# Sums of down-projection weights held behind an addition of a later unit, and spread over fourteen units

## The chip, the cores and the metric

One NeuronCore of a Trainium2 chip runs the whole kernel as one launch. The metric is the device time of that launch in microseconds. The kernel before takes 1783.04 us, the median of three runs (1782.25 to 1786.08).

## What is computed

One layer of a decoder on 1024 tokens of width 1024, in float32: a norm and a combined projection, two attention branches, their gated sum, a SwiGLU block with 2816 hidden features, a gated embedding and a last norm. The change lies in the SwiGLU block:

```python
n2 = rms_norm(h, g_ffn[i])
h = h + (jax.nn.silu(n2 @ w_ffn_gate[i]) * (n2 @ w_ffn_up[i])) @ w_ffn_down[i]
```

## The kernel before

Every product in float32 is made of three matmuls on a high and a low half of each operand (`passes`, lines 134 to 139: high by high, high by low, low by high). `split` (lines 130 to 132) makes the halves: ScalarE casts the high half (line 131), VectorE subtracts it from the source to give the low half (line 132). So the third matmul of a product, line 139, is the first that needs VectorE's work on that weight.

The SwiGLU block uses the Winograd form of a 2 by 2 block product: seven products of sums of blocks in place of eight. For the gate and up projections the hidden features come in 22 units of 256, here numbered 0 to 21: even ones are columns of the gate, odd ones the same columns of the up projection. `wino` builds a unit: GpSimd makes the sums of weight blocks (`s1`, and in place in `raw`; lines 958, 959, 975, 977), each of the seven weight operands is split into a tile `wl` (three buffers), and each of the seven products i is a group of twelve matmuls into a bank of PSUM named `pP`, `pR` or `pQ`. Behind a group, ScalarE copies the bank (`snap`) or VectorE adds it to an earlier copy (`add`, line 968). From unit 3 on the products come in the order 1, 5, 2, 6, 7, 3, 4; the addition behind product 7 reads `pP`, that behind product 3 reads `pQ`.

A gate unit ends in SiLU on ScalarE. An up unit multiplies (GpSimd at line 1023, or VectorE at line 1025), and then VectorE makes four subtractions for the down projection (`sub`, line 1016), which wait for GpSimd's product; all seven results go to DRAM (`d_g`, line 1013). The first three units work on operands `b` that VectorE still splits at the stage's start.

The down projection runs after the 22 units and needs, for each of its eleven block rows kk (KK is 11), four sums of weight blocks too. They are made during the units: `down_in(kk)` loads four blocks of 128 by 512 into one half of the buffer `spare` (line 1102, four DMAs of 256 KB), and `down_sums(kk)` makes the four sums on VectorE (line 1109), each followed by a store to DRAM (`d_w`, line 1110). The two halves of `spare` alternate, so the load of block kk + 2 waits for the stores of block kk. Earlier, `spare` holds other tiles. At the end, eight direct blocks are loaded into it (line 1131).

All these loads and stores are issued from SP's queue, where the loads of the units' raw weights (line 830, 1 MB each, three buffers) and the stores of `d_g` stand too. The code calls `down_in` in one turn of a loop over units 3 to 21 and `down_sums` in the next, but the order of the code is not the order of issue: a scheduler that works with modelled times puts each instruction on its engine's list as soon as what it needs is there, unless a priority or `tc.issue_after` says otherwise.

Of the kernel before, what the change touches and what calls it, by code (L numbers as in the profile page):

```python
# [14 lines left out]
ALU = mybir.AluOpType  # L15
# [36 lines left out]
def decoder_layer(ctx: ExitStack, tc: tile.TileContext, x, p, positions, g_mix, w_in, g_q_a, w_q_b,  # L52
                  g_kv_a, w_kv_b, w_br_mla, w_br_sb, w_out, g_ffn, w_ffn_gate, w_ffn_up, w_ffn_down,
                  w_ple_gate, w_ple_proj, g_ple, g_final, xT, pT, out):
    nc = tc.nc
# [101 lines left out]
    with ExitStack() as att:  # L157
# [17 lines left out]
        with ExitStack() as sb:  # L175
# [111 lines left out]
            with ExitStack() as p2:  # L287
# [18 lines left out]
                kk = rp.tile([P, S], F32, name="kk")  # L306
# [28 lines left out]
            for k2 in range(NK // 2):  # L335
# [4 lines left out]
                for t in range(NT):  # L340
                    s = slice(t * P, (t + 1) * P)
# [135 lines left out]
            for pr in range(HEADS // 2):  # L477
                kst, q1, q2 = cur
                oT = wp.tile([P, S], F32, name="oT", tag="oT", bufs=1)
                for a in range(2):  # L480
# [5 lines left out]
                                            op=ALU.subtract)  # L486
# [346 lines left out]
    def gate_up_raw(u):  # L833
        return raw_unit((w_ffn_gate, w_ffn_up)[u % 2], u // 2)
# [111 lines left out]
    t1_factors(quarter[0], bc0)  # L946
    acc = out_group(1, 2, 2)

    FIRST = (1, 2, 5, 6, 7, 3, 4)
    firsts = iter((M, O, B))  # L950
    ORDER = (1, 5, 2, 6, 7, 3, 4)

    def wino(raw, order, ctile, ready):

        a11, a12, a21, a22 = [raw[:, kh * 4:kh * 4 + 4, f * P:(f + 1) * P] for f in range(2) for kh in range(2)]
        s1 = wk.tile([P, 4, P], F32, name="s1", tag="c", bufs=4)
        G = nc.gpsimd
        G.tensor_tensor(out=s1, in0=a21, in1=a22, op=ALU.add)
        G.tensor_tensor(out=a21, in0=a11, in1=a21, op=ALU.subtract)
        left = {1: a11, 2: a12, 3: a12, 4: a22, 5: s1, 6: a11, 7: a21}  # L960
        bank, s = {}, {}

        def snap(key, pt):
            s[key] = ctile()
            nc.scalar.copy(out=s[key], in_=pt)

        def add(key, pt):
            nc.vector.tensor_tensor(out=s[key], in0=pt, in1=s[key], op=ALU.add)  # L968
            return s[key]

        for n, i in enumerate(order):
            w = wk.tile([P, 2, 4, P], F32R, name="wl", tag="wl", bufs=3)
            split(w[:, 0], w[:, 1], left[i])
            if i == 1:
                G.tensor_tensor(out=a11, in0=s1, in1=a11, op=ALU.subtract)
            elif i == 2:
                G.tensor_tensor(out=a12, in0=a12, in1=a11, op=ALU.subtract)
            k = "P" if i in (1, 6, 7, 4) else "R" if i == 2 else "Q"
            first = k not in bank
            if first:  # L980
                spec = B if k == "R" else next(firsts) if k == "Q" and order is FIRST else A
                bank[k] = ps.tile([P, HALF], F32, name="p" + k, **spec)
            pt = bank[k]
            passes(pt, [((w[:, 0, kk, :], w[:, 1, kk, :]), (Bn[i][:, 0, kk, :], Bn[i][:, 1, kk, :]))
                        for kk in range(4)], first=first, last=i in (2, 3, 4), skip_group_check=True)
            if i in (1, 6):
                snap(i, pt)
            elif i == 2:
                ready(0, 0, add(1, pt))
            elif i == 3:  # L990
                ready(0, 1, add(6, pt))
            elif i == 4:
                ready(1, 0, None, pt)
            elif (12 - i) in s:
                ready(1, 1, add(12 - i, pt))
            else:
                snap(i, pt)
            yield
# [80 lines left out]
    def rest():  # L1079
        global_sl = sl  # L1080
        nxt = gate_up_raw(3)
        for u in range(3, NFF):
            raw = nxt
            if u + 1 < NFF:
                nxt = gate_up_raw(u + 1)
            if u % 2:
                yield up_unit(u // 2, raw, ORDER, t_tile, global_sl)
            else:
                global_sl = {}
                yield gate_unit(raw, ORDER, t_tile, global_sl)  # L1090

    KK = NFF // 2
# [5 lines left out]
    def down_in(kk):  # L1098

        a = {(f, kh): spare[:, 4 * (kk % 2) + 2 * f + kh, :] for f in range(2) for kh in range(2)}  # L1100
        for (f, kh), t in a.items():
            nc.sync.dma_start(out=t, in_=down_block(f, kh, kk))
        return a

    def down_sums(kk, a):

        for i, dst, x, y, op in ((5, (1, 1), (1, 0), (1, 1), ALU.add), (7, (1, 0), (0, 0), (1, 0), ALU.subtract),
                                 (6, (0, 0), (1, 1), (0, 0), ALU.subtract), (3, (0, 1), (0, 1), (0, 0), ALU.subtract)):
            nc.vector.tensor_tensor(out=a[dst], in0=a[x], in1=a[y], op=op)
            nc.sync.dma_start(out=d_w[LEFT[i], kk], in_=a[dst])  # L1110
# [2 lines left out]
    DIRECT = {1: (0, 0), 2: (0, 1), 4: (1, 1)}  # L1113
    before = None
    blocks = {}
    for n, u in enumerate(rest()):

        if 2 <= n < KK + 2:
            blocks[n - 2] = down_in(n - 2)
        for _ in range(2):  # L1120
            next(u)
        for _ in before or ():
            pass
        for _ in range(3):
            next(u)
        before = u
        if 3 <= n < KK + 3:
            down_sums(n - 3, blocks.pop(n - 3))
        if n == KK + 4:
            for kk in range(0, 8, 2):  # L1130
                nc.sync.dma_start(out=spare[:, kk:kk + 2, :], in_=wd[0, :, kk:kk + 2, hcol(0)])

# [75 lines left out]
    for hf, c0, n in ((1, 0, 4), (0, 0, 2), (0, 2, 2)):  # L1208
        c = slice(c0 * P, (c0 + n) * P)
        w_ = slice(0, n * P)  # L1210
        s = slice(hf * HALF + c0 * P, hf * HALF + (c0 + n) * P)
# [67 lines left out]
```

## Time and profile before

| | |
|---|---|
| time, median of three runs | 1783.04 us |
| the profiled execution | 1785.67 us |
| its span, first to last instruction | 1784.0 us |
| mean granted clock of TensorE | 0.981 |
| TensorE busy (matmuls) | 1697.2 us, 95% |
| VectorE busy | 1157.2 us, 65% |
| ScalarE busy | 901.7 us, 51% |
| GpSimd busy | 389.7 us, 22% |
| gate and up units | about 1000 to 1451 us of the span |

In the profile PE is TensorE, PEld its weight loads, DVE VectorE, ACT ScalarE, POOL GpSimd and SP the queue of SyncE. A line such as L1109 is a line of the kernel. A row of a timeline gives the start in the span, the duration, the engine, the line, the operation, and out<-in with sizes; brackets give the idle time ahead of it and what ended it. In the view of waits a row gives the waiting instruction, what it waited for, the total in us, the times and the longest. The clock is a share of full speed.

### The profile page before, as it was taken

The page shows a single profiled execution, that of the slowest core. Times are in us where ns is not written, and L with a number is a line of the kernel's source. Part 1 is how long each engine was busy: PE and PEld are TensorE (multiplying, and loading weights), DVE is VectorE, ACT ScalarE, POOL GpSimd, SP SyncE. Part 2 cuts the span into 40 slices and gives each one's busy share as a digit, 9 for nine tenths or more (in the row PEclk, how much of TensorE's full clock was granted, in tenths as well). Part 3 has the DMA queues.
Part 4 walks back from the last instruction along what each step waited for, and adds up shares of the span by engine and source line. Part 5 has one row for each costly group of instructions (what it writes and reads, how often), then busy time and mean ns, then how long its engine had stood idle before and what let it go on. Part 6 is the DMA issues. An engine that isn't in the chain of part 4 may idle for free.

```text
span 1784.0 us, 23325 instructions
## 1 busy us (share of the span) xinstructions
PE 1697.2 (95%) x8148; PEld 1410.5 (79%) x8148; DVE 1157.2 (65%) x2063; ACT 901.7 (51%) x1748; POOL 389.7 (22%) x401
## 2 busy tenths in 40 slices
PE   6999999999998999996999899899999999999996
PEld 5888878888786888885889777688888878887795
DVE  6667788778885766686468765754444545557656
ACT  5266676767774777775335633233333334445411
POOL 2011320000210533342202623334434310000000
PEclk9999999999999999998999899999999999999998
DMA  5212221213314210215953475853223328565522
GB/s 171 55 58 48 59 60 42 82 45 90 115 42 138 72 61 31 83 58 200 346 205 115 143 257 180 277 168 100 95 89 118 113 101 300 191 198 164 165 67 79
DMA packets 168249, 222.16 MB, mean 125 GB/s; under 512 B 23170, under 2 KB 99970, under 8 KB 168130
## 3 DMA queue, kind: packets, MB, share of 16 engines
q1 hardware_dynamic: 162098, 200.73, 34.6%
q0 software_dynamic: 6032, 19.93, 3.1%
q8 instruction: 64, 1.05, 0.2%
q14 instruction: 55, 0.45, 0.1%
HBM read 151.93 MB, written 67.90 MB: 123 GB/s over the span
## 4 chain that ended last, share of the span: by engine, by line
PE 74%; DVE 9%; issue 6%; DMA 5%; POOL 2%; ACT 2%; SPq 1%; POOLq 0%; DVEq 0%; ACTq 0%
PE pt L137 5%; PE pt L138 5%; PE pt L139 5%; PE pd L138 4%; PE pd L137 4%; PE pd L139 4%; PE pP L139 3%; PE pP L137 3%; PE pP L138 3%; DMA spare<-w_ffn_down 2%; PE po L137 2%; PE tp L651 2%; PE po L138 2%; PE po L139 2%; PE pg L139 2%
## 5 line engine op out<-in xcount | busy, mean ns | idle before, releaser
L137 PE MATMUL pt<-nTh,w_h 128*128 128x512 f32 (+1 forms) x480 | 192.5, 402 | 3.4 <-ACT go L355 2.4
L138 PE MATMUL pt<-nTl,w_h 128*128 128x512 f32 (+1 forms) x480 | 190.1, 396 | 0.0
L139 PE MATMUL pt<-nTh,w_l 128*128 128x512 f32 (+1 forms) x480 | 189.0, 395 | 0.0
L132 DVE TENSOR_TENSOR wl<-raw,wl 128x512 fp32r<-128x512 f32 x132 | 95.4, 723 | 101.9 <-ACT wl L131 101.4
L139 PE MATMUL pP<-b,wl 128*128 128x512 f32 x352 | 139.8, 399 | 10.1 <-DVE wl L132 10.1
L131 ACT CAST wl<-raw 128x512 fp32r<-128x512 f32 x132 | 82.0, 622 | 129.2 <-PE pP L139 59.0
L137 PE MATMUL pP<-b,wl 128*128 128x512 f32 x352 | 140.2, 398 | 5.0 <-DVE t L968 3.2
L138 PE MATMUL pP<-b,wl 128*128 128x512 f32 x352 | 139.3, 396 | 0.0
L137 PEld LDWEIGHTS pt<-nTh,w_h 128*128 128x128 f32 (+1 forms) x480 | 90.7, 189 | 26.1 <-ACT go L355 5.8
L139 PEld LDWEIGHTS pt<-nTh,w_l 128*128 128x128 f32 (+1 forms) x480 | 90.6, 189 | 19.7
L138 PEld LDWEIGHTS pt<-nTl,w_h 128*128 128x128 f32 (+1 forms) x480 | 90.9, 189 | 18.5
L138 PE MATMUL pd<-drs,dls 128*128 128x512 f32 x296 | 102.0, 390 | 1.0 <-DVE drs L132 1.0
L139 PE MATMUL pd<-drs,dls 128*128 128x512 f32 x296 | 101.7, 389 | 0.0
L132 DVE TENSOR_TENSOR drs<-drr,drs 128x512 fp32r<-128x512 f32 x74 | 50.8, 690 | 78.1 <-ACT drs L131 78.1
L137 PE MATMUL pd<-drs,dls 128*128 128x512 f32 x296 | 100.7, 392 | 0.4 <-ACT dls L131 0.4
L131 ACT CAST drs<-drr 128x512 fp32r<-128x512 f32 x74 | 45.9, 623 | 105.0 <-PE pd L139 98.3
L637 POOL TENSOR_SCALAR pw<-pw,st 128x128 f32<-128x128 f32 (+5 forms) x48 | 75.0, 1569 | 71.6 <-DVE st L633 20.2
L139 PEld LDWEIGHTS pP<-b,wl 128*128 128x128 f32 x352 | 67.4, 192 | 28.2 <-DVE wl L132 13.9
L137 PEld LDWEIGHTS pP<-b,wl 128*128 128x128 f32 x352 | 67.7, 192 | 20.1 <-DVE t L968 4.1
L138 PEld LDWEIGHTS pP<-b,wl 128*128 128x128 f32 x352 | 67.6, 192 | 14.3
L445 DVE TENSOR_TENSOR sz<-sz,T 128x512 f32<-128x512 f32 (+2 forms) x96 | 52.2, 550 | 34.6 <-PE T L443 33.8
L356 POOL DMA_DIRECT2D d_gate<-go x32 | 17.8, 556 | 260.3 <-ACT go L355 221.2
(371 smaller groups left out, 4821.9 us busy)
## 6 DMA issues: line engine op xcount, KB each, us to landing
d_g<-t SPq DMA_DIRECT2D x74, 256.0 KB, 2.0
drr<-d_g SPq DMA_DIRECT2D x74, 256.0 KB, 2.8
w_raw<-w_in SPq DMA_DIRECT2D x33, 512.0 KB, 4.2
raw<-w_ffn_gate SPq DMA_DIRECT2D x11, 1024.0 KB, 5.6
raw<-w_ffn_up SPq DMA_DIRECT2D x11, 1024.0 KB, 5.5
spare<-w_ffn_down SPq DMA_DIRECT2D x44, 256.0 KB, 3.7
d_w<-spare SPq DMA_DIRECT2D x44, 256.0 KB, 3.6
drr<-d_w SPq DMA_DIRECT2D x44, 256.0 KB, 2.6
```

Source lines behind the costliest of these rows:

```text
L131: nc.scalar.copy(out=h, in_=src)
L132: eng.tensor_tensor(out=l, in0=src, in1=r32(h), op=ALU.subtract)
L137: nc.tensor.matmul(ps, lhsT=ah, rhs=bh, start=first and i == 0, stop=False, **kw)
L138: nc.tensor.matmul(ps, lhsT=ah, rhs=bl, start=False, stop=False, **kw)
L139: nc.tensor.matmul(ps, lhsT=al, rhs=bh, start=False, stop=last and i == n - 1, **kw)
L356: nc.gpsimd.dma_start(out=dst, in_=go[0:rows, :])
L445: nc.vector.tensor_tensor(out=sz[:, c0:], in0=sz[:, c0:], in1=T[:, c0:], op=ALU.subtract)
L637: nc.gpsimd.tensor_scalar(out=pw[:, 0:nk], in0=pw[:, 0:nk], scalar1=st[:, 6:7], scalar2=None, op0=ALU.mult)
L651: nc.tensor.transpose(tp[:, i * P:(i + 1) * P], rows[i][:, kb * P:(kb + 1) * P], ident)
```

## The change

The four sums of a block are no longer free to be issued when their loads have landed: they are held behind the latest addition (`add`) that the code had made at that point, which is the one behind product 7 of the unit of that turn. And the blocks are called in at other turns: n counts the turns from 0 (unit 3), and the new table `when` puts the loads of kk = 0 to 10 at turns 2, 3, 4, 5, 7, 8, 9, 10, 12, 13, 14, and the sums one turn later, in place of turns 2 to 12 and 3 to 13. The last loads into `spare` are called one turn later. The kernel gets three lines longer, so lines behind the first edit have moved by one, and those behind the loop by three.

```diff
+    latest = {}
...
         def add(key, pt):
-            nc.vector.tensor_tensor(out=s[key], in0=pt, in1=s[key], op=ALU.add)
+            latest["add"] = nc.vector.tensor_tensor(out=s[key], in0=pt, in1=s[key], op=ALU.add).ins
             return s[key]
...
+    when = {2 + 5 * kk // 4: kk for kk in range(KK)}
     for n, u in enumerate(rest()):
-        if 2 <= n < KK + 2:
-            blocks[n - 2] = down_in(n - 2)
+        if n in when:
+            blocks[when[n]] = down_in(when[n])
...
-        if 3 <= n < KK + 3:
-            down_sums(n - 3, blocks.pop(n - 3))
-        if n == KK + 4:
+        if n - 1 in when:
+            with tc.issue_after(latest["add"]):
+                down_sums(when[n - 1], blocks.pop(when[n - 1]))
+        if n == KK + 5:
```

What it moves is seen in the engines' lists. First VectorE in units 0 to 2, up to the split for product 2 of unit 1, `wl_9915` (`b3` is an operand, `pR_9900` the bank of unit 0). Before:

```order
L132 TENSOR_TENSOR b3_9246<-t_9047,b3_9246 128x512
L1109 TENSOR_TENSOR spare_9084<-spare_9084 128x512
L132 TENSOR_TENSOR b3_9246<-t_9051,b3_9246 128x512
L132 TENSOR_TENSOR b3_9246<-t_9055,b3_9246 128x512
L968 TENSOR_TENSOR spare_9084<-pR_9900,spare_9084 128x512
L132 TENSOR_TENSOR b3_9246<-t_9059,b3_9246 128x512
L1109 TENSOR_TENSOR spare_9084<-spare_9084 128x512
L132 TENSOR_TENSOR wl_9915<-raw_9706,wl_9915 128x512
```

And now:

```order
L132 TENSOR_TENSOR b3_9246<-t_9047,b3_9246 128x512
L132 TENSOR_TENSOR b3_9246<-t_9051,b3_9246 128x512
L132 TENSOR_TENSOR b3_9246<-t_9055,b3_9246 128x512
L969 TENSOR_TENSOR spare_9084<-pR_9900,spare_9084 128x512
L132 TENSOR_TENSOR b3_9246<-t_9059,b3_9246 128x512
L132 TENSOR_TENSOR wl_9915<-raw_9706,wl_9915 128x512
```

The two sums ahead of that split are gone. The same goes for all sums in units 0 to 5: on VectorE's list the first sum now stands behind the addition after product 7 of unit 6.

Second, VectorE in unit 7, an up unit, from its addition behind product 7 (`t_10882<-pP_10851`; `t_10953<-pQ_10869` is that behind product 3, `t_11044` the first subtraction, `t_10916` the product at line 1025). Before:

```order
L968 TENSOR_TENSOR t_10882<-pP_10851,t_10882 128x512
L132 TENSOR_TENSOR wl_11052<-raw_10686,wl_11052 128x512
L132 TENSOR_TENSOR wl_11072<-raw_10838,wl_11072 128x512
L968 TENSOR_TENSOR t_10953<-pQ_10869,t_10953 128x512
L132 TENSOR_TENSOR wl_11091<-raw_10838,wl_11091 128x512
L1025 TENSOR_TENSOR t_10916<-pP_10851,t_10916 128x512
L1016 TENSOR_TENSOR t_11044<-t_10730,t_10811 128x512
L132 TENSOR_TENSOR wl_11108<-raw_10838,wl_11108 128x512
```

And now:

```order
L969 TENSOR_TENSOR t_10882<-pP_10851,t_10882 128x512
L1110 TENSOR_TENSOR spare_9084<-spare_9084 128x512
L132 TENSOR_TENSOR wl_11052<-raw_10686,wl_11052 128x512
L1110 TENSOR_TENSOR spare_9084<-spare_9084 128x512 x3
L132 TENSOR_TENSOR wl_11072<-raw_10838,wl_11072 128x512
L969 TENSOR_TENSOR t_10953<-pQ_10869,t_10953 128x512
L132 TENSOR_TENSOR wl_11091<-raw_10838,wl_11091 128x512
L1017 TENSOR_TENSOR t_11044<-t_10730,t_10811 128x512
L1026 TENSOR_TENSOR t_10916<-pP_10851,t_10916 128x512
L1017 TENSOR_TENSOR t_10811<-t_10811,t_10712 128x512
L132 TENSOR_TENSOR wl_11108<-raw_10838,wl_11108 128x512
```

Four sums have come in behind the addition, and two subtractions now stand ahead of the split `wl_11108`. On both lists the other subtractions, the addition on the next unit's `pR` and the split for product 1 of unit 9 follow. Units 6, 8, 9, 11, 12, 13, 14, 16, 17 and 18 hold a block's sums at the same place.

Third, GpSimd in unit 7 (`t_10811` is the product for which the first subtraction waits, `raw_11133` the weights of unit 10). Before:

```order
L1023 TENSOR_TENSOR t_10730<-t_10730,t_10882 128x512
L977 TENSOR_TENSOR raw_10838<-raw_10838 128x4x128
L958 TENSOR_TENSOR s1_11282<-raw_11133 128x512
L1023 TENSOR_TENSOR t_10811<-t_10811,t_10953 128x512
L959 TENSOR_TENSOR raw_11133<-raw_11133 128x4x128
```

And now:

```order
L1024 TENSOR_TENSOR t_10730<-t_10730,t_10882 128x512
L978 TENSOR_TENSOR raw_10838<-raw_10838 128x4x128
L1024 TENSOR_TENSOR t_10811<-t_10811,t_10953 128x512
L959 TENSOR_TENSOR s1_11278<-raw_11133 128x512
L960 TENSOR_TENSOR raw_11133<-raw_11133 128x4x128
```

The product now stands ahead of the first sum on newly loaded weights; in units 9, 11, 13 and 17 too. On SP's list the loads into `spare` and the stores of `d_w`, which stood together around the loads for units 3 to 9, now stand between the loads for units 9 to 21, as a rule one store ahead of such a load and three behind it. TensorE's list is the same from unit 3 to unit 21.

## The prediction

> **What bounds the kernel now.** I read the time by stage first (the view of windows), then who waited for whom on TensorE, then the instructions around each wait. The stage that the change touches is the gate and up projections, from about 1000 to 1451 us of the span; the change moves nothing before it. Each row gives the length, then busy time and count of PE, PEld, DVE, ACT and POOL, then the granted clock, the DMA share and GB/s.
>
> ```profile
> core 0 of [0], span 1784.0 us
> core 0: us, PE busy (x) PEld busy (x) DVE busy (x) ACT busy (x) POOL busy (x), PEclk, DMA share, GB/s
> 1005.00:1175.00 170.00, 150.96 (x627) 121.61 (x626) 113.60 (x154) 62.69 (x114) 63.06 (x41) 0.95 0.67 224
> 1175.00:1451.00 276.00, 273.06 (x1198) 223.85 (x1196) 129.38 (x178) 98.39 (x170) 103.51 (x74) 1.00 0.29 97
> 1020.31:1024.75 4.44, 4.44 (x11) 3.48 (x11) 4.44 (x8) 0.00 (x0) 4.41 (x1) 0.50 0.49 172
> 1062.72:1065.88 3.16, 3.15 (x8) 2.48 (x9) 3.12 (x4) 0.00 (x0) 1.59 (x1) 0.50 0.87 252
> 1130.24:1134.22 3.98, 3.98 (x10) 3.12 (x11) 3.91 (x4) 0.00 (x0) 2.78 (x2) 0.57 0.43 161
> 1153.82:1158.03 4.21, 4.21 (x12) 3.31 (x12) 3.41 (x4) 0.19 (x1) 1.67 (x1) 0.60 0.91 351
> 1160.00:1180.00 20.00, 20.00 (x90) 16.57 (x89) 10.26 (x15) 7.77 (x14) 7.22 (x5) 1.00 0.65 212
> ```
>
> In the second part of the stage TensorE works 273 of 276 us at full clock: it is the bound. In the first part it stands idle for 19 of 170 us and four times falls to about half clock. Who it waits for there, and in the second part (total, times, longest), stands in the view of waits:
>
> ```profile
> PE pP L139 <- DVE wl L132: 7.2, 3, 4.0
> PE pR L139 <- DVE wl L132: 5.8, 1, 5.8
> PE pP L137 <- DVE t L968: 3.2, 2, 2.5
> PE pP L137 <- DVE spare L968: 1.8, 1, 1.8
> ```
>
> ```profile
> PE pP L139 <- DVE wl L132: 2.9, 6, 0.9
> ```
>
> So in the first part it waits 18.0 us for VectorE, for the low half of a weight (`wl`) or for an addition that frees a bank, and in the second 2.9 us in six places. VectorE in turn waits, in the first part, for this:
>
> ```profile
> DVE spare L1109 <- DMA spare<-w_ffn_down: 25.8, 13, 6.1
> ```
>
> ```profile
> L1109 DVE TENSOR_TENSOR spare<-spare x44: 678/692/1769, 1016.0 to 1165.2; 128x512 f32<-128x512 f32 x44
> ```
>
> All 44 sums run between 1016.0 and 1165.2 us. The rows below show VectorE working through its list in the written order, so a sum whose load has not landed holds up the splits and additions behind it. Next the matmuls that waited, each with its idle time in brackets:
>
> ```profile
> 1020.31 0.80 PE L139 MATMUL pR<-b,wl 128*128 128x512 f32 x1 [5.76 <-DVE wl L132]
> ...
> 1051.72 0.50 PE L137 MATMUL pP<-b,wl 128*128 128x512 f32 x1 [1.75 <-DVE spare L968]
> ...
> 1062.72 0.79 PE L137 MATMUL pP<-b,wl 128*128 128x512 f32 x1 [2.51 <-DVE t L968]
> ...
> 1073.39 0.50 PE L137 MATMUL pP<-b,wl 128*128 128x512 f32 x1 [0.72 <-DVE t L968]
> ...
> 1125.62 0.39 PE L137 MATMUL pP<-b,wl 128*128 128x512 f32 x1
> 1125.85 0.39 PE L138 MATMUL pP<-b,wl 128*128 128x512 f32 x1
> 1130.24 0.50 PE L139 MATMUL pP<-b,wl 128*128 128x512 f32 x1 [4.00 <-DVE wl L132]
> 1130.58 0.49 PE L137 MATMUL pP<-b,wl 128*128 128x512 f32 x1
> ...
> 1153.82 0.50 PE L139 MATMUL pP<-b,wl 128*128 128x512 f32 x1 [2.64 <-DVE wl L132]
> ...
> 1194.22 0.50 PE L139 MATMUL pP<-b,wl 128*128 128x512 f32 x1 [0.41 <-DVE wl L132]
> ```
>
> A matmul starts 0.23 us after the one before (1125.62, 1125.85). From 1125.85 to 1130.58 are two steps, 4.73 us in place of 0.46: 4.27 lost where the bracket says 4.00. I add this 0.27 to each bracket. And VectorE ahead of those waits:
>
> ```profile
> 1015.96 0.69 DVE L1109 TENSOR_TENSOR spare<-spare 128x512 f32<-128x512 f32 x1 [0.58 <-DMA spare<-w_ffn_down]
> 1016.57 1.29 DVE L132 TENSOR_TENSOR b<-t,b 128x512 fp32r<-128x512 f32 x2
> ...
> 1018.97 0.68 DVE L1109 TENSOR_TENSOR spare<-spare 128x512 f32<-128x512 f32 x1
> 1019.58 0.68 DVE L132 TENSOR_TENSOR wl<-raw,wl 128x512 fp32r<-128x512 f32 x1
> ...
> 1047.68 2.17 DVE L1109 TENSOR_TENSOR spare<-spare 128x512 f32<-128x512 f32 x3 [4.09 <-DMA spare<-w_ffn_down]
> ...
> 1059.62 1.25 DVE L1109 TENSOR_TENSOR spare<-spare 128x512 f32<-128x512 f32 x1 [6.05 <-DMA spare<-w_ffn_down]
> ...
> 1128.30 0.69 DVE L1109 TENSOR_TENSOR spare<-spare 128x512 f32<-128x512 f32 x1 [3.52 <-DMA spare<-w_ffn_down]
> ...
> 1139.04 0.73 DVE L1109 TENSOR_TENSOR spare<-spare 128x512 f32<-128x512 f32 x1 [1.19 <-DMA spare<-w_ffn_down]
> ...
> 1152.49 0.68 DVE L1109 TENSOR_TENSOR spare<-spare 128x512 f32<-128x512 f32 x1
> 1153.09 0.68 DVE L132 TENSOR_TENSOR wl<-raw,wl 128x512 fp32r<-128x512 f32 x1
> ...
> 1162.51 2.15 DVE L1109 TENSOR_TENSOR spare<-spare 128x512 f32<-128x512 f32 x3 [0.40 <-DMA spare<-w_ffn_down]
> ```
>
> **What the change takes away.** In the new order the first sum comes behind the fourth addition of unit 6, so units 0 to 5 hold none. Their stalls, one by one:
>
> - 1020.31: two sums and 0.58 us of waiting go from ahead of the split (each 0.61 from its start to the next: 1015.96 to 1016.57, 1018.97 to 1019.58), 0.58 + 0.61 + 0.61 = 1.8 us. The rest of this stall is twelve and more splits of the operands `b`, and stays. The half clock behind it stays too: if it ended at the same time, 0.9 of the 1.8 would be given back; if it lasted as long as behind the other stalls (3.2 to 4.2 us, not 4.44), up to 0.6 would come on top. Bounds 0.9 to 2.4; I take 1.8.
> - 1051.72: the addition that frees the bank stood behind three sums that waited 4.09. 1.75 + 0.27 = 2.0, all of it.
> - 1062.72: behind a sum that waited 6.05. 2.51 + 0.27, and 3.16 us at clock 0.50, so 1.6 more: 4.4. Bounds 2.8 (clock still halved for some other reason) to 4.4; I take 4.4.
> - 1073.39: 0.99. It ends a row of additions that also wait for a product of GpSimd, so it may remain: 0 to 1.0, I take 0.5.
> - 1130.24: behind a sum that waited 3.52. 4.27, and 3.98 us at 0.57, 1.7 more: 6.0. Bounds 4.3 to 6.0; I take 6.0.
> - 1153.82: unit 5. 2.64 + 0.27, and 4.21 us at 0.60, 1.7 more: 4.6. A unit of this kind without sums has 0.68 at 1194.22 (0.41 + 0.27), which I leave: 3.9. Bounds 2.2 to 4.6. The 0.6 that is left of the 7.2 us (7.2 - 4.0 - 2.6) is the same gap in unit 3, and stays.
>
> Together 1.8 + 2.0 + 4.4 + 0.5 + 6.0 + 3.9 = 18.6 us.
>
> That a half clock follows gaps as short as 2.5 to 2.6 us is read from the rows at 1062.72 and 1153.82. The Trainium skill, "TensorE: Matmul & The Clock Gate", section "HAM oscillation — how this bites in real kernels", gives as its rule no gaps above about 3.4 us; by it these two would have kept the full clock, and the sum would be 1.6 + 1.7 = 3.3 us smaller. This trace disagrees, with 0.50 and 0.60 granted behind those gaps, so I go by the rows.
>
> **What it puts elsewhere.** The sums now lie behind the fourth addition of units 6, 7, 8, 9, 11, 12, 13, 14, 16, 17 and 18: one, then a split, then three. Queued behind them on VectorE are a split, the fifth addition and more splits; TensorE waits for those.
>
> Gate units (6, 8, 12, 14, 16, 18): nothing. Before, four sums lie in unit 6 too (1162.51 and the one after it), and TensorE has no gap in 1160 to 1180 (20.00 of 20.00, x90). Splits there are ready a whole group of twelve matmuls, 2.7 us, early; without that cover each block would cost up to 4 x 0.69 = 2.8.
>
> Up units (7, 9, 11, 13, 17): these end in the chain product of GpSimd, four subtractions, split, which already costs the six gaps of the second part: 2.9 + 6 x 0.27 = 4.5, 0.75 each. The new order of unit 7 is, instruction for instruction, that of unit 5 before, on VectorE and on GpSimd, but for two things: there the first sum waited 1.19 for its load, and another sum (0.60) stood ahead of the last split. The loads now come a full block ahead, right behind the stores of the block two before. So the gap should be 2.64 - 1.19 - 0.60 = 0.85, with 0.27 1.12 us: 0.37 more than now, five times, 1.9 us. Bounds: none at all (-3.7, since GpSimd's product no longer queues behind a weight load) to the 4.6 of unit 5 in each (+19).
>
> SP's queue: the weights of a unit load behind one store of a sum instead of a whole block's. They have time:
>
> ```profile
> 1181.17 0.37 SPq L830 DMA_DIRECT2D raw<-w_ffn_gate  x1
> ```
>
> ```profile
> 1210.47 0.62 ACT L131 CAST wl<-raw 128x512 fp32r<-128x512 f32 x1 [1.66 <-issue]
> ```
>
> The load issued at 1181.17 feeds its first cast at 1210.47, 29 us later; a store that waits for a sum delays it by 2 to 3 us. The stores of `d_g` behind the new loads wait no longer than for one transfer. The prefetch into `spare` for the down projection moves behind the last block, three units before it is read. All three: nothing. If that cover were gone, ten loads would be late.
>
> Net gain 18.6 - 1.9 = 16.7 us of span. The profiled execution took 1785.67 us, 1.67 more than its span and 2.63 more than the median of the runs; I take the gain off the median: 1783.04 - 16.7 = 1766.3. The hold is seen in the order itself, so that it does nothing is no rival.
>
> **Rivals.**
>
> - A shared path. Here is GpSimd beside VectorE in unit 7:
>
> ```profile
> 1189.27 1.77 DVE L1016 TENSOR_TENSOR t<-t 128x512 f32<-128x512 f32 x1 [0.62 <-POOL t L1023]
> ```
>
> This subtraction took 1.77 where such an instruction takes 0.69. If each up unit loses one such stretch more, 5 x 1.08 = 5.4 go: 1771.7. Against it: unit 5, from which I priced, has stretched instructions already. The Trainium skill, "GPSIMD Engine Reference", section "1. Specifications", speaks against the change in the same way: it says that GpSimd's way to SBUF is shared with VectorE and contended by instructions with two SBUF inputs, which the sums are. The 1.77 agrees. Chance 0.11.
> - The three first units stay slow. With the sums gone, 1051.72, 1062.72 and 1073.39 are made late by the subtractions that wait for GpSimd: 2.0 + 4.4 + 0.5 less, 1773.2. For: the last of them is such a place. Against: the long waits ahead are those for loads. Chance 0.09.
> - No change. Each up unit stalls as unit 5 did, clock included: 5 x 4.6 - 3.7 = 19.3 against 18.6, 1783.7. Against: 1.19 and 0.60 of that stall have causes that are gone. Chance 0.05.
> - Slower: VectorE becomes the bound of a unit. It is the case from the point where a held sum delays a split past its group, in gate and up units alike; then 44 x 0.69 = 30.4 us come onto the path against 18.6: 1794.8. Against: VectorE is busy 129 of 276 us, and would be 160. Chance 0.05.
>
> **How the numbers follow.** The forecast has 0.70. Its own bounds: low ends together give a gain of 0.9 + 2.0 + 2.8 + 0 + 4.3 + 2.2 = 12.2 less some 4, 1775; high ends 2.4 + 2.0 + 4.4 + 1.0 + 6.0 + 4.6 and 3.7 give 24, 1759, which needs all at once; I cut it at 1761. The range 1761 to 1775 takes in the first two rivals and leaves out the others and the tails. Faster by over 0.2% (3.6 us, about what a measurement here can tell): 0.90. Within: 0.05. Slower: 0.05.
>
> **What would show it.** In the new profile VectorE's wait for `spare<-w_ffn_down` is near 0, sums run from some 1145 to some 1380, the stalls of 1051 to 1154 are gone with their half clock, and the stall near 1020 is about 4 us. Five gaps of about 0.85 in the up units show the price right; gaps above 2.5 with a half clock, or gaps in gate units, show it wrong. A first part that keeps its idle time would show the whole reading wrong.

## The result, and the profile after

The changed kernel takes 1773.97 us, the median of eight runs (1765.8 to 1778.46), against 1783.04 of the kernel before (eight runs, 1779.95 to 1787.08). The ratio is 0.9943, 95% interval 0.9922 to 0.9964: some 9 us faster. The profiled execution took 1773.21 us with a span of 1771.5, which is 12.5 below the span before.

The same two stretches in the view of windows (length, then busy time and count of PE, PEld, DVE, ACT and POOL, granted clock, DMA share, GB/s):

```profile
1005.00:1175.00 170.00, 163.09 (x709) 133.32 (x708) 95.89 (x130) 68.17 (x122) 68.85 (x46) 0.99 0.36 121
1175.00:1451.00 276.00, 265.54 (x1154) 216.47 (x1152) 159.29 (x214) 96.28 (x167) 101.39 (x69) 0.99 0.50 169
```

In the first stretch TensorE is busy for 12 us more than before and runs at 0.99 of its clock. In the second it lost 7.5 us of busy time (part of that because the stage now ends 11 us earlier, inside the stretch). Whom it waited for in the first stretch (two single waits of 1.1 and 0.5 us are left out):

```profile
PE pR L139 <- DVE wl L132: 3.9, 1, 3.9
PE pP L139 <- DVE wl L132: 1.4, 2, 0.9
```

And in the second:

```profile
PE pP L139 <- DVE wl L132: 8.2, 6, 2.0
```

Six waits again in the second, as before, but 8.2 us in place of 2.9. VectorE's waits for the loads into `spare` (25.8 us before) have left the view. The sums, in the view of tiles, and the matmuls that waited for VectorE (two are left out: unit 3 at 1097.93 with 0.52, unit 13 at 1298.55 with 1.44):

```profile
L1110 DVE TENSOR_TENSOR spare<-spare x44: 676/689/693, 1143.1 to 1385.9; 128x512 f32<-128x512 f32 x44
```

```profile
1018.81 0.79 PE L139 MATMUL pR<-b,wl 128*128 128x512 f32 x1 [3.88 <-DVE wl L132]
...
1064.47 0.50 PE L137 MATMUL pP<-b,wl 128*128 128x512 f32 x1 [0.52 <-DVE t L969]
...
1137.20 0.50 PE L139 MATMUL pP<-b,wl 128*128 128x512 f32 x1 [0.87 <-DVE wl L132]
...
1177.07 0.50 PE L139 MATMUL pP<-b,wl 128*128 128x512 f32 x1 [1.50 <-DVE wl L132]
...
1216.79 0.50 PE L139 MATMUL pP<-b,wl 128*128 128x512 f32 x1 [1.35 <-DVE wl L132]
...
1257.12 0.77 PE L139 MATMUL pP<-b,wl 128*128 128x512 f32 x1 [1.95 <-DVE wl L132]
...
1337.42 0.50 PE L139 MATMUL pP<-b,wl 128*128 128x512 f32 x1 [0.46 <-DVE wl L132]
...
1377.34 0.50 PE L139 MATMUL pP<-b,wl 128*128 128x512 f32 x1 [1.53 <-DVE wl L132]
```

The long stalls of the first units are gone, but for the part of the first one that was to stay (3.88 at 1018.81). From 1137.20 on the rows are the up units 5, 7, 9, 11, 15 and 17, and unit 13: the five that hold sums have gaps of 1.35 to 1.95 us, unit 15, which holds none, 0.46. No gate unit has a gap.

**The account.** The same matmuls serve as marks in both traces.

| stretch | before | after | gained |
|---|---|---|---|
| first wait (1013.82; 1014.19) to the stall behind it (1020.31; 1018.81) | 6.49 | 4.62 | 1.87 |
| to the gap of unit 5 (1153.82; 1137.20) | 133.51 | 118.39 | 15.12 |
| to the gap of unit 7 (1194.22; 1177.07) | 40.40 | 39.87 | 0.53 |
| to the first wait of the down projection (1451.77; 1440.44) | 257.55 | 263.37 | -5.82 |
| to the end of the span | 332.23 | 331.06 | 1.17 |

In the third row the gap of unit 7 grew from 0.41 to 1.50 although the row got 0.53 shorter, so 1.62 was gained there: the half clock behind unit 5. The gain is 1.87 + 15.12 + 1.62 = 18.6 us, and the new cost 1.09 + 5.82 = 6.9. With 1.2 from the end and 0.4 lost ahead of the stage that makes the 12.5. The median moved less because the profiled execution before lay 2.6 above its median and the one after 0.8 below.

Why a gap is 1.5 us is seen on VectorE in unit 7, from the addition behind product 7:

```profile
1161.56 0.69 DVE L969 TENSOR_TENSOR t<-pP,t 128x512 f32<-128x512 f32 x1 [0.89 <-PE pP L139]
1162.16 0.68 DVE L1110 TENSOR_TENSOR spare<-spare 128x512 f32<-128x512 f32 x1
1162.76 1.78 DVE L132 TENSOR_TENSOR wl<-raw,wl 128x512 fp32r<-128x512 f32 x1
1164.46 2.13 DVE L1110 TENSOR_TENSOR spare<-spare 128x512 f32<-128x512 f32 x3
1166.51 0.68 DVE L132 TENSOR_TENSOR wl<-raw,wl 128x512 fp32r<-128x512 f32 x1
```

And on GpSimd at the same time:

```profile
1162.33 1.66 POOL L1024 TENSOR_TENSOR t<-t 128x512 f32<-128x512 f32 x1 [5.14 <-DVE t L969]
1167.34 1.29 POOL L978 TENSOR_TENSOR raw<-raw 128x512 f32<-128x512 f32 x1 [3.35 <-DVE wl L132]
1168.59 1.74 POOL L1024 TENSOR_TENSOR t<-t 128x512 f32<-128x512 f32 x1
```

The split at 1162.76 took 1.78 us where the next one took 0.68: it lies across GpSimd's product (1162.33 to 1163.99) and ends 0.55 behind it, as if it had begun only then. So the second split starts 4.95 us behind the addition. In unit 15, without sums, it starts 3.86 behind it (1326.81 and 1322.95), and waited last for ScalarE's cast:

```profile
1322.95 0.69 DVE L969 TENSOR_TENSOR t<-pP,t 128x512 f32<-128x512 f32 x1 [0.89 <-PE pP L139]
1323.61 0.69 DVE L132 TENSOR_TENSOR wl<-raw,wl 128x512 fp32r<-128x512 f32 x1
1326.81 0.69 DVE L132 TENSOR_TENSOR wl<-raw,wl 128x512 fp32r<-128x512 f32 x1 [2.51 <-ACT wl L131]
```

GpSimd's `L978` waits for that second split, the product of the chain stands behind `L978`, the subtractions wait for that product, and TensorE waits for the split behind them.

The stretching is no single case. Between 1080 and 1440 us of this profile every split and every subtraction shown by itself that starts inside a GpSimd instruction with over 0.2 us of it left ends 0.54 to 0.56 us behind that instruction: it takes 1.78 with 1.23 us left, 1.47 with 0.92 left, 0.99 with 0.44 left. With 0.1 or less left it takes 0.69.

### The profile page after: what moved, and what is told of

It is laid out like the page before. It is cut to its first block, busy times and chain, and to the rows that moved or that the text cites. A ratio compares the mean times of both kernels' runs of the same rounds, so it can differ in the third digit from the quotient of the medians.

```text
span 1771.5 us, 23317 instructions
## 1 busy us (share of the span) xinstructions
PE 1691.8 (96%) x8148; PEld 1407.6 (79%) x8148; DVE 1162.9 (66%) x2063; ACT 901.8 (51%) x1748; POOL 390.6 (22%) x401
## 4 chain that ended last, share of the span: by engine, by line
PE 77%; DVE 9%; issue 7%; DMA 3%; ACT 2%; POOL 2%; SPq 0%; POOLq 0%; DVEq 0%; ACTq 0%
PE pt L137 5%; PE pt L138 5%; PE pt L139 5%; PE pd L137 4%; PE pd L138 4%; PE pP L139 4%; PE pd L139 4%; PE pP L137 3%; PE pP L138 3%; PE po L137 2%; PE tp L651 2%; PE po L138 2%; PE po L139 2%; PE pQ L138 2%; PE pQ L137 2%
## 5 line engine op out<-in xcount | busy, mean ns | idle before, releaser
L132 DVE TENSOR_TENSOR wl<-raw,wl 128x512 fp32r<-128x512 f32 x132 | 108.2, 820 | 104.8 <-ACT wl L131 104.3
```

Source lines behind the costliest of these rows:

```text
L132: eng.tensor_tensor(out=l, in0=src, in1=r32(h), op=ALU.subtract)
```

## The experiments

The theories: W, the sums and what they collide with on VectorE make the gaps; O, the new order of the chain (two subtractions ahead of a split) makes them; T, the transfers of the blocks make the raw weights late. Later C: what counts is that VectorE and GpSimd shut each other out. And L: where GpSimd's sum on newly loaded weights stands ahead of the product of the chain, a late load holds up the chain. The column "late part" is the stretch of the fourth row above, from unit 7's gap to the down projection's first wait, from the one profiled execution. Ratios are to the kernel before on the same chip; kernels between two empty rows shared its runs. A difference of a few us between two profiles is not all of the edit's making: the two profiles of the changed kernel itself reach the first wait of the stage at 1014.19 and 1017.41. So stretches say more here than medians.

| kernel | median us | ratio, 95% | gaps of the five units | late part |
|---|---|---|---|---|
| after_again | 1771.4 | 0.9929 (0.9909 to 0.9950) | 1.35 to 1.94 | 261.83 |
| order_only | 1769.3 | 0.9912 (0.9888 to 0.9937) | 0.52 or below 0.3 | 259.73 |
| no_moves | 1768.53 | 0.9915 (0.9889 to 0.9941) | 1.32 to 1.35 | 260.56 |
| alt_hold | 1782.9 | 0.9991 (0.9973 to 1.0009) | 1.10 to 5.25 | 267.92 |
| | | | | |
| behind_split | 1773.29 | 0.9957 (0.9945 to 0.9968) | 1.52 | 261.63 |
| behind_split_product | 1769.78 | 0.9934 (0.9921 to 0.9947) | 1.51 to 1.52 | 261.58 |
| hold_only | 1771.1 | 0.9939 (0.9927 to 0.9951) | 1.35 to 1.93 | 263.17 |
| spread_only | 1784.44 | 1.0015 (1.0002 to 1.0027) | no sums there | 256.30 |
| | | | | |
| product_dve | 1767.18 | 0.9907 (0.9886 to 0.9927) | 0.58 to 0.69 | 257.90 |
| product_dve_first | 1766.8 | 0.9899 (0.9878 to 0.9920) | 0.58 to 0.73 | 258.11 |
| gates_product | 1765.56 | 0.9898 (0.9876 to 0.9920) | 0.52 | 257.61 |
| | | | | |
| gates_six | 1766.81 | 0.9924 (0.9901 to 0.9947) | 0.52 | 257.61 |

**after_again**, without an edit.

> The changed kernel unchanged, as the measure for the other runs of this chip. All theories: ratio to the kernel before between 0.992 and 0.997, five gaps of 1.3 to 2.0 us on TensorE between 1175 and 1385 us, in up units that hold sums, and one of about 0.5 in the up unit without sums.

As expected, but for one thing: unit 5, which holds no sums, has a gap of 2.07 here where it had 0.87. behind_split_product comes back to it. The cost in the up units, counted as above, is 1.16 in unit 7 and 4.28 behind it: 5.4 us here, for 6.9.

**order_only.** The sums of the five up units go; the order of all else is pinned (`behind(key)` issues what follows behind the instruction noted under that key).

```diff
-            nc.vector.tensor_tensor(out=a[dst], in0=a[x], in1=a[y], op=op)
+            if sums:
+                nc.vector.tensor_tensor(out=a[dst], in0=a[x], in1=a[y], op=op)
...
-                down_sums(when[n - 1], blocks.pop(when[n - 1]))
+                down_sums(when[n - 1], blocks.pop(when[n - 1]), n % 2 == 1)
...
+        with behind("product"):
             G.tensor_tensor(out=s1, in0=a21, in1=a22, op=ALU.add)
...
+              with behind(("sub", 7)):
                 nc.vector.tensor_tensor(out=g, in0=pt, in1=g, op=ALU.mult)
...
+        with behind(("sub", 4)):
             next(u)
...
+        with behind(("sub", 5)):
             next(u)
```

> Leaves out the sums of the five up units 7, 9, 11, 13 and 17 (their blocks are stored unsummed), and pins every other instruction of VectorE, GpSimd and TensorE to the order of the changed kernel. Theory W (the work of the sums on VectorE, and the collision with GpSimd's product that it brings, makes the gap): the five gaps fall from 1.35 to 1.95 us to 0.5 or less, as in the unit without sums (0.46); with restart and half clock the five cost 10.7 us now and would cost 5 x 0.72 = 3.6 or less, so about 7 us faster than the changed kernel. Theory O (the order that came with the sums, with a subtraction and a product ahead of the splits, makes it): gaps stay between 1.0 and 1.5, time within 2 us of the changed kernel. Theory T (transfers make the raw weights late): gaps stay as they are.

The timeline of TensorE, at the gaps of units 7 and 15:

```profile
1179.98 0.50 PE L140 MATMUL pP<-b,wl 128*128 128x512 f32 x1 [0.52 <-DVE wl L133]
...
1337.66 0.50 PE L140 MATMUL pP<-b,wl 128*128 128x512 f32 x1 [3.40 <-DVE wl L133]
```

The gaps of the five fell to 0.52 or out of sight in the same order: O is out, W holds. The median fell by 2.1 us against after_again, not by 7, and the intervals overlap: unit 15, where nothing was edited, now had a gap of 3.40. GpSimd shows why:

```profile
1330.15 1.28 POOL L966 TENSOR_TENSOR s<-raw 128x512 f32<-128x512 f32 x1 [3.92 <-DMA raw<-w_ffn_gate]
1331.39 1.30 POOL L1033 TENSOR_TENSOR t<-t 128x512 f32<-128x512 f32 x1
```

In that unit the sum on newly loaded weights still stands ahead of the product of the chain, and its load came late: issued at 1321.62, behind the prefetch into `spare` that had moved ahead of it, it let GpSimd start 8.5 us after that issue. So T has a place too, in units of the old order.

**no_moves.** No load of a block, no store of a sum.

```diff
-        for (f, kh), t in a.items():
-            nc.sync.dma_start(out=t, in_=down_block(f, kh, kk))
...
-            nc.sync.dma_start(out=d_w[LEFT[i], kk], in_=a[dst])
...
-                lw = raw_in(d_w[LEFT[i], kk])
+                lw = raw_in(down_block(0, 0, kk))
```

> Leaves out the loads of the blocks into spare and the stores of the sums, so that the sums are made of what lies in the buffer; the down projection reads unsummed blocks from the weights in place of the stored sums. All 44 sums and the order of VectorE and GpSimd are as in the changed kernel. Theories W and O: the five gaps stay at 1.3 to 2.0 us and the time of this part within 1 us. Theory T: the raw weights come earlier, the gaps fall below 0.9, some 4 to 7 us faster.

```profile
1173.70 0.50 PE L139 MATMUL pP<-b,wl 128*128 128x512 f32 x1 [1.32 <-DVE wl L132]
```

The gaps stay at 1.32 to 1.35: they are not made by transfers. But they no longer scatter up to 1.95, units 3, 5 and 15 show none above 0.3, and the late part is 1.3 to 2.8 us shorter than in the two profiles of the changed kernel. So W, with a smaller share of T on top; 1.3 us is a little more than the 1 us that W had allowed. How the share of T arises is seen in unit 11 (1.95 and 1.94 with the transfers, 1.35 without). With them GpSimd's sum on new weights waits 1.24 for its load, then falls beside the chain's end on VectorE: a split and a subtraction of 1.78 each (1251.77, 1253.48 in the changed kernel). In no_moves they are a subtraction of 1.18 and a split of 1.77 (1247.81, 1248.92). The 0.6 us are the difference: a late load costs time there by moving a GpSimd instruction into VectorE's way.

**alt_hold.** In up units the sums go behind the next unit's addition on `pR`.

```diff
+            if key == 1:
+                latest["second"] = latest["add"]
...
-            with tc.issue_after(latest["add"]):
+            with tc.issue_after(latest["second" if n % 2 == 0 else "add"]):
```

> All work is done; in the up units the four sums are held behind the addition of product 2 of the next unit, that is past the chain of subtractions, in the gate units behind the addition of product 7 as in the changed kernel. Theories W and O: the five gaps fall to 0.4 to 0.8 us, the time by 5 to 7 us against the changed kernel, to a ratio near 0.991. Theory T: gaps and time stay, since the same transfers are made. A loss of its own: if the sums now delay splits of the next gate unit, new gaps of 0.5 to 2 us stand behind the place.

A miss: the time is that of the kernel before. With the sums gone from that place, the scheduler put GpSimd's list back into the old order, and the load of the weights, behind more traffic, came late. GpSimd in unit 13, and TensorE behind it:

```profile
1298.42 1.29 POOL L959 TENSOR_TENSOR s<-raw 128x512 f32<-128x512 f32 x1 [5.80 <-DMA raw<-w_ffn_gate]
1299.66 1.29 POOL L1026 TENSOR_TENSOR t<-t 128x512 f32<-128x512 f32 x1
```

```profile
1305.90 0.80 PE L139 MATMUL pP<-b,wl 128*128 128x512 f32 x1 [5.25 <-DVE wl L132]
```

That load was issued at 1288.73, behind three loads of a block. A wait of that kind accounts for all five gaps: in each of these units GpSimd's sum waits for a DMA, and the gap is that wait less 0.5 us (waits 2.10, 2.00, 1.61, 5.80, 2.31, gaps 1.59, 1.51, 1.10, 5.25, 1.80; in unit 15, without sums, 0.76 and 0.26). So at their new place the sums show no cost of their own; the old order of GpSimd's list is what made the gaps. Of the 6.8 us between this span and that of after_again 6.1 lie in the late part.

**behind_split.** In the five up units the first sum, too, goes behind the split for product 4, with GpSimd's order pinned to that of the changed kernel. For that the code calls the sums a turn later; two of the blocks (kk 1 and 4) have then been overwritten by later blocks, so those sums are of other data, in the same number and with no wait of VectorE for a load.

```diff
+            if i == 4:
+                latest["split"] = low
...
+        if held:
+            with tc.issue_after(latest["split"]):
+                down_sums(*held.pop())
```

> All work is done. In the five up units 7, 9, 11, 13 and 17 the one sum that stood ahead of the split for product 4 stands behind it, with the other three; nothing else changes on VectorE, GpSimd and TensorE. Theory W, collision: the split starts with the addition's end again, as where no sums stand, and GpSimd's product collides with sums instead; the next split then comes 0.66 + 4 x 0.61 + 1.1 = 4.2 us behind the addition, in place of 4.95 now and 3.86 without sums, so the gaps fall from about 1.5 to 0.6 to 0.9 us, and the time by 3 to 6 us against the changed kernel. Theory W, plain work (four sums cost the same wherever they stand in the unit): gaps stay above 1.2, time within 1.5 us of the changed kernel.

```profile
1162.29 0.69 DVE L976 TENSOR_TENSOR t<-pP,t 128x512 f32<-128x512 f32 x1 [0.89 <-PE pP L140]
1162.94 0.69 DVE L133 TENSOR_TENSOR wl<-raw,wl 128x512 fp32r<-128x512 f32 x1
1163.55 3.96 DVE L1121 TENSOR_TENSOR spare<-spare 128x512 f32<-128x512 f32 x4
1167.43 0.68 DVE L133 TENSOR_TENSOR wl<-raw,wl 128x512 fp32r<-128x512 f32 x1
```

Missed: all five gaps are 1.52. The first split is quick again (0.69), but the sums then take 3.96 in place of 4 x 0.61 = 2.44: the collision moved to them and cost 1.5. Its place in the row is not what counts. By the numbers as written plain work had won; but plain work, six instructions of 0.61 (3.7 us), would end before the cast at 3.86. To tell the two apart the product itself had to go.

**behind_split_product.** The same, and GpSimd's product ahead of its sum on new weights in all up units.

```diff
-                if j in (3, 4, 5, 6, 8) and (f, t) == (0, 1):
+                if (f, t) == (0, 1):
                     latest["prod"] = ins
```

> As behind_split, and in all up units, 3, 5, 15, 19 and 21 too, GpSimd's product stands ahead of its first sum on the newly loaded weights, as it does in the units with sums. Theory L (where that sum stands ahead of the product, a weight load that lands late holds up the chain): units 3, 5 and 15 have no gap above 0.6 us, and the time is 1 to 3 us below behind_split. Without L: those units keep gaps of 0.4 to 2, time within 1 us of behind_split.

Units 3, 5 and 15 have 0.52, 0.54 and 0.52, where behind_split had 2.07 in unit 5; 3.5 us faster in the medians. Unit 15 had 0.54 there too and unit 3 under 0.3, so it is unit 5 alone that speaks for L. And of the 3.4 us between the two spans only 1.2 lie between the stall near 1018 and unit 5's gap; 1.4 lie ahead of that stall and 0.7 behind the units. So L holds for unit 5, and is worth 1.2 us here.

**hold_only** and **spread_only**, the two halves of the change.

```diff
-    when = {2 + 5 * kk // 4: kk for kk in range(KK)}
+    when = {2 + kk: kk for kk in range(KK)}
...
-        if n == KK + 5:
+        if n == KK + 4:
```

```diff
-            with tc.issue_after(latest["add"]):
-                down_sums(when[n - 1], blocks.pop(when[n - 1]))
+            down_sums(when[n - 1], blocks.pop(when[n - 1]))
```

> The hold alone: the blocks keep their eleven turns in a row, so the sums lie in units 6 to 16, five of them up units again (7, 9, 11, 13 and 15). If the spread is worth nothing, the first part is free of stalls as in the changed kernel, five gaps of about 1.5 us stand in those units, and the ratio to the kernel before is 0.992 to 0.996. If the spread is needed (loads of every unit crowd the queue and make the raw weights late), gaps of 2 us and more with a half clock, and a ratio above 0.997.

> The spread alone: the turns of the changed kernel without the hold, so the sums go to VectorE's list as soon as their loads are modelled to have landed, the first of them in units 0 to 2 again. If the hold is what brings the gain: waits of VectorE for the loads into spare of 10 us and more, stalls on TensorE before 1160 us, and a ratio of 0.997 to 1.003. If the spread brings part of it: a ratio of 0.994 to 0.997.

The hold alone gives 0.9939, the changed kernel 0.9943 and 0.9929: the spread adds nothing that can be measured. The spread alone gives no gain (1.0015); VectorE's wait for the blocks is back:

```profile
DVE spare L1110 <- DMA spare<-w_ffn_down: 26.0, 12, 6.1
```

**product_dve.** The product that collides moves to VectorE, in the five units.

```diff
-                nc.gpsimd.tensor_tensor(out=g, in0=g, in1=u, op=ALU.mult)
+                eng = nc.vector if j in HELD and (f, t) == (1, 1) else nc.gpsimd
+                eng.tensor_tensor(out=g, in0=g, in1=u, op=ALU.mult)
```

> All work is done. In the five up units with sums (7, 9, 11, 13, 17) the product that GpSimd made right behind the addition after product 7 is made by VectorE, so that VectorE has one instruction more there (0.61 us) and GpSimd one less; one of the four sums slips behind the next split, nothing else changes. Theory C (VectorE and GpSimd shut each other out, and the 1.1 to 1.5 us that VectorE loses to that product make the split late): the split is on time again, 3.86 us behind the addition, the five gaps fall from 1.5 to about 0.5 us, the time by 4 to 7 us against the changed kernel. Theory W (VectorE's own work makes it late): one more instruction, gaps of 1.5 to 2.1 us, time the same or up to 3 us more.

VectorE in unit 7:

```profile
1161.23 0.69 DVE L970 TENSOR_TENSOR t<-pP,t 128x512 f32<-128x512 f32 x1 [0.89 <-PE pP L139]
1161.83 0.68 DVE L1112 TENSOR_TENSOR spare<-spare 128x512 f32<-128x512 f32 x1
1162.43 0.69 DVE L132 TENSOR_TENSOR wl<-raw,wl 128x512 fp32r<-128x512 f32 x1
1163.03 0.68 DVE L1026 TENSOR_TENSOR t<-t 128x512 f32<-128x512 f32 x1
1163.64 1.41 DVE L1112 TENSOR_TENSOR spare<-spare 128x512 f32<-128x512 f32 x2
1165.08 0.69 DVE L132 TENSOR_TENSOR wl<-raw,wl 128x512 fp32r<-128x512 f32 x1
```

```profile
PE pP L139 <- DVE wl L132: 3.5, 6, 0.7
```

VectorE does the same work and a product more, and is on time: the second split starts 3.85 behind the addition, and the wait of the late stretch (1175 to 1440) falls from 8.2 to 3.5 us. From the addition on, six instructions stand ahead of that split, as many as in the changed kernel (addition, split and four sums there; addition, split, product and three sums here), and it starts 1.1 us earlier. C holds, and W as plain work is out. One of the four sums moved behind that split; ahead of it, it would have made the split 0.4 to 0.6 us late (seven instructions of 0.61, or one more 0.6 behind these rows), about half of the 1.1 of the changed kernel, with an instruction more. The ratio is 0.9907, for 0.9943 and 0.9929 of the changed kernel on other chips: 4 to 6 us faster by the medians, though the intervals overlap. The late part, 257.90 for 263.37 and 261.83, says the same.

**product_dve_first** joins the two edits, of product_dve and behind_split_product.

> As product_dve, and in every up unit, 3, 5, 15, 19 and 21 too, GpSimd's remaining product stands ahead of its first sum on newly loaded weights. By what behind_split_product showed, units 3, 5 and 15 then have 0.5 us each and no longer up to 2.1: 0 to 3 us below product_dve, a ratio near 0.990.

Units 3, 5 and 15 have 0.52 each. The time is level with product_dve: its own profile showed no long gap there to begin with, so there was nothing there for the second edit to remove.

**gates_product.** All sums in gate units, two blocks in two of them, and the product first. The loads of block 0 stand ahead of the last readers of the tiles they overwrite, so some values are not the reference's.

```diff
-    when = {2 + 5 * kk // 4: kk for kk in range(KK)}
+    at = (1, 3, 5, 5, 7, 9, 11, 11, 13, 15, 17)
...
-        if n - 1 in when:
-            with tc.issue_after(latest["add"]):
-                down_sums(when[n - 1], blocks.pop(when[n - 1]))
+        for kk in range(KK):
+            if n == at[kk]:
+                with tc.issue_after(latest["add"]):
+                    down_sums(kk, blocks.pop(kk))
```

> All work is done. All sums are held in gate units, where they stand behind the addition of product 7 with no product of GpSimd right behind it: one block in units 4, 6, 10, 12, 16, 18 and 20, two in units 8 and 14; and GpSimd's product stands ahead of its first sum on newly loaded weights in every up unit. Theory C: no up unit has a gap above 0.6, as in order_only without its late unit; 4 to 7 us below the changed kernel, ratio near 0.990. Units 8 and 14 hold eight sums, 4.9 us, against a cover of 2.7 us, and may cost up to 2.2 us each. If sums cost the same in any unit: gaps of 1 us or more in gate units, time within 2 us of the changed kernel.

The up units 3 to 17 all have 0.52, and no gate unit has a gap, not even the two that hold eight sums.

**gates_six**, the same with nothing overwritten; three gate units hold eight sums.

```diff
-    at = (1, 3, 5, 5, 7, 9, 11, 11, 13, 15, 17)
+    at = (3, 3, 5, 7, 7, 9, 11, 11, 13, 15, 17)
```

> All work is done, and no load stands ahead of a reader of what it overwrites. As gates_product, but the blocks lie in the gate units 6, 8, 10, 12, 14, 16, 18 and 20, two each in 6, 10 and 14. By theory C and by gates_product: gaps of 0.5 us in all up units, none in gate units, 4 to 7 us below the changed kernel, a ratio of 0.988 to 0.992, level with product_dve_first within 2 us. If the eight sums of a gate unit outlast its cover: gaps of 0.5 to 2 us in units 6, 10 and 14.

```profile
1173.49 0.50 PE L140 MATMUL pP<-b,wl 128*128 128x512 f32 x1 [0.52 <-DVE wl L133]
```

```profile
PE pP L140 <- DVE wl L133: 2.6, 5, 0.5
```

The late part is 257.61, as in gates_product and within 0.1 of the kernel before, whose late part holds no sums at all. So the 36 sums that lie in that stretch cost nothing, in gate units and with the product first, and the eight of unit 6 leave no gap either. The median, 1766.81, is level with product_dve_first; their intervals overlap, and which is the better stays open. Both are faster than the kernel before. That they also beat the changed kernel is shown by the late part (257.61 and 258.11 for 263.37 and 261.83), not by the ratios: that of gates_six, 0.9924, lies within the interval of the changed kernel.

## Why the prediction was right and where it was wrong

- **What the change takes away: right in mechanism and in size.** Forecast 18.6 us, measured 18.6; the agreement to the tenth is luck. The stall at 1020.31 gave 1.87 for 1.8; from there to unit 5's gap 15.1 were forecast (2.0 + 4.4 + 0.5 + 6.0, and 2.64 - 0.41) and 15.12 came; the half clock behind unit 5 gave 1.6 for 1.7. Within the 15.1 some terms offset each other: that at 1062.72 left 0.52, unit 5 kept 0.87 and not 0.41, and 1073.39 went whole where half was taken. In after_again, with 2.07 left in unit 5, the same marks give 17.5. The stalls at 1051.72 and 1073.39 left no row, so the rival "the three first units stay slow" is out.
- **Up units: wrong in size, by a step that was wrong in kind.** The step that failed is "So the gap should be 2.64 - 1.19 - 0.60 = 0.85", five times, 1.9 us. The gaps were 1.35 to 1.95, the cost 6.9. The 1.19 that the first sum of unit 5 waited for its load was not lost on top of the rest: during it GpSimd's product ran alone. The rows of before, VectorE:

```profile
1137.16 0.69 DVE L968 TENSOR_TENSOR t<-pP,t 128x512 f32<-128x512 f32 x1 [0.91 <-PE pP L139]
...
1139.70 0.68 DVE L132 TENSOR_TENSOR wl<-raw,wl 128x512 fp32r<-128x512 f32 x1
...
1142.36 0.68 DVE L132 TENSOR_TENSOR wl<-raw,wl 128x512 fp32r<-128x512 f32 x1
```

  and GpSimd:

```profile
1137.93 1.30 POOL L1023 TENSOR_TENSOR t<-t 128x512 f32<-128x512 f32 x1 [4.92 <-DVE t L968]
```

  There the product took 1.30 and the split behind the wait 0.68. Without the wait the two meet, and the split takes 1.78. The second split came 5.20 us behind the addition there (1142.36 and 1137.16) and 4.95 now: of 1.19 taken away only 0.25 arrived. The other term held: from the second split to the gap it was 11.46 us and is now 10.56, 0.90 less for the 0.60 of the sum that left. Subtracting a wait from a row is right only if nothing else used the time.
- **The rival "a shared path" came true** inside the likeliest case: the cost was 5.0 us more than forecast, for its 5.4 (3.5 more in after_again, so that its price fits so well is partly luck). It was given 0.11 on the ground that unit 5 "has stretched instructions already". It had, at other places; not at this one. product_dve shows the mechanism. What the Trainium skill, "GPSIMD Engine Reference", section "1. Specifications", says of the way to SBUF shared with VectorE agrees with these rows (1.78 us for 0.68).
- **Of the 6.9**, 4.4 us is idle time of units 9 to 17 beyond before's, 1.1 that of unit 7, and the 1.4 that is left is about the price of the half clock behind one gap (3 us at 0.51). no_moves puts some of it down to transfers: its late part is 2.8 shorter, with that half clock among the 2.8.
- **Gate units: right.** No gap there, and gates_six shows room for eight sums.
- **SP's queue: half wrong.** The prediction called the cast, 29 us behind the issue, the load's first reader. GpSimd's sum reads it first, in unit 7 before at 1186.68, 5.5 us behind the issue. That cover is thin, and alt_hold and order_only show it gone (5.80 and 3.92 us of waiting). The changed kernel was spared most of it because the product moved ahead of that sum, which the prediction counted only as a bound.
- **The spread** is worth nothing that these runs can tell; the prediction gave it no term.
- **The median.** The whole gain was taken off the median, though the profiled execution lay 2.6 us above it, so 16.7 forecast stands against 11.7 by the same marks in the traces and 9.1 in the medians. The 1773.97 lies 7.7 us above the forecast of 1766.3 and only 1 us below the upper end of the range. The range reached that far for the low ends of all terms together and for two rivals. One of these came true, so that the time fell inside is owed to that width and not to the sum.
- "Slower, VectorE becomes the bound" and "no change" are out: no gate unit has a gap, and the five up units cost 6.9, not 19. The gaps of 1.35 to 1.95 lie between the two signs that the prediction named, 0.85 for its price and over 2.5 against it.

## What to carry to other kernels

Holding background work behind a fixed point pays where it had been queued with its load not yet there: look for an engine's wait for a transfer whose result nobody needs yet. Then choose the place of the work by what GpSimd does at that moment, where the work is VectorE's, and not by idle time alone: here four sums of 0.61 us fitted into 2.5 idle us, and still made 1.1 us of delay, since a GpSimd product fell into the same stretch. Two remedies removed that delay: moving the product to VectorE, and moving the sums to units where no product follows. When a stall is taken apart into terms, ask of each wait what ran during it.

## What the hardware showed that was not expected

**VectorE and GpSimd shut each other out for whole instructions.** Without sums the first split (1323.61) was there before the product (1323.72) and stayed at 0.69, and the product took 1.73:

```profile
1323.72 1.73 POOL L1024 TENSOR_TENSOR t<-t 128x512 f32<-128x512 f32 x1 [5.14 <-DVE t L969]
```

In unit 7 the product came first and the split took 1.78. The one that starts second is stretched by about what is left of the other: the product by 0.44 where 0.58 of the split was left, the split by 1.10 where 1.23 of the product was left. Moving the product to VectorE, for one more instruction there, made the late part 4 to 5.5 us shorter.

**A half clock does not follow from the length of a gap alone.** Behind the gap of 1.95 in unit 11 of the changed kernel the granted clock was 0.51 (view of windows):

```profile
1257.12:1259.00 1.88, 1.88 (x5) 1.49 (x6) 1.42 (x1) 0.39 (x1) 1.27 (x1) 0.51 1.04 393
```

Behind the gap of 3.40 in order_only it was full:

```profile
1337.66:1340.00 2.34, 2.33 (x10) 1.93 (x11) 1.76 (x2) 1.01 (x3) 1.68 (x1) 1.00 0.45 163
```

after_again kept 1.00 behind 1.94 and 2.07, hold_only fell to 0.57 behind 1.99, alt_hold to 0.50 behind 5.25. In spread_only alone 0.54 followed a gap of 2.04 us (at 1051.13) and 1.00 one of 2.20 (at 1072.86). What decides between 1.9 and 3.4 us these runs do not show. The Trainium skill, "TensorE: Matmul & The Clock Gate", section "HAM oscillation — how this bites in real kernels", draws its line at about 3.4 us; the 0.51 and 0.57 behind gaps of 1.95 and 1.99 disagree. Half clocks may be part of why executions of the changed kernel scatter over 12 us: the four longest ran at mean clocks of 0.980 to 0.982, the two shortest at 0.986 and 0.987. No run tests it.
